# Three modulation blocks of the first mixer on VectorE, a fourth in the second mixer

## The chip, the cores and the metric

One NeuronCore of a Trainium2 chip runs the whole program, in one launch. The metric is the time of one execution in microseconds of device time, from the median of the runs. The engines are called TensorE (PE in the profile, PEld its weight loads), VectorE (DVE), ScalarE (ACT), GpSimd (POOL) and SyncE (SP, which here only issues transfers). Each takes its own instructions in the order of the program; they wait for one another through semaphores.

## The reference

A block of two layers over 512 latent tokens and 256 context tokens of 1024 channels, in float32. The first layer mixes the tokens by a bidirectional gated delta rule, the second by a short gated convolution; behind each stands a mixture of 32 experts. Ahead of every part the tokens are normalised and modulated: shift, scale and gate come from one matrix-vector product a layer, the "modulation", with a matrix of 1024 x 6144.

```python
def ada_params(cond, w, b):
    m = jax.nn.silu(cond) @ w + b
    return jnp.split(m[..., None, :], N_MOD, axis=-1)

def reference(x, c, ctx, c_ctx, ada_w, ada_b, ...):
    for i in range(DEPTH):
        sh_m, sc_m, gt_m, sh_f, sc_f, gt_f = ada_params(c, ada_w[i], ada_b[i])
        ...
        h = modulate(x, norm_mix[i], sh_m, sc_m)
        if kind == 0:
            y, yc = deltanet_mixer(h, hc, w_in_a[j], conv_a[j], ...)
        else:
            y = shortconv_mixer(h, w_in_b[j], conv_b[j], w_out_b[j], rows)
        x = x + gt_m * y
        hf = modulate(x, norm_ffn[i], sh_f, sc_f).reshape(b * s, d)
        x = x + gt_f * hier_moe(hf, router_g[i], router_e[i], w1[i], w3[i], w2[i]).reshape(b, s, d)
    return rmsnorm(x, final_norm)
```

The six vectors of a layer are three blocks of 2048 columns: block 0 is shift and scale of the mixer, block 1 the mixer's gate and the experts' shift, block 2 the experts' scale and gate. Block (l, b) is block b of layer l. Block (0, 0) is needed first and for both token kinds; it is not touched here. The other five are needed later: (0, 1) and (0, 2) at the end of the first mixer and in the first experts, (1, 0) at the entry of the second mixer, (1, 1) and (1, 2) at its end and in the last experts.

## The kernel before

The program is one long sequence: start-up (to about 60 us), phase A of the first mixer (projections of 32 "jobs" of 128 columns each, to about 400 us), its recurrence and output projection (to about 590 us), the first experts (to about 1090 us), the second mixer (about 1136 to 1360 us) and the last experts.

All weights come in units of 2 MB through rings of slots. `plan` writes the order of the units by hand, and `issue` starts a load on SP's queue as soon as the slot's last unit counts as used up; a load therefore waits on the engine that used the slot.

A job of phase A takes four columns' worth of a unit, splits 128 columns of the weights into a high and a low part (`split`: ScalarE writes `whi`, L637; GpSimd subtracts for `wlo`, L639), multiplies them in three passes with the tokens (`mm3`, L654, into the banks `pj` and `pc`), convolves the result along the tokens on VectorE and ScalarE (`job_conv`, L768 to L770) and, for k and v, turns it (`job_post`, L803, with sums of squares on ScalarE, L808). Between the matmuls of a job `work` puts in pieces of the "side work" of the delta rule: the matrices L (`lmat`, L897 to L908), the inverses of their diagonal blocks (`lanes`, on VectorE and GpSimd in turn: L931 and L932 step by step, then L948 and L949), and the whole inverses (`tmat`). There are three sets of lanes, one for each pair of token tiles. `norms` (L818) stands ahead of the first L.

In phase A the modulation of four blocks, (0, 1), (0, 2), (1, 0) and (1, 1), is done on TensorE (`ada_block`, L253): a unit is 256 rows of the matrix by 2048 columns, 8 matmuls with the condition as the stationary operand, which the profile shows as 16 records. `ada_at` gives the number of units at each job: 16 units over jobs 4 to 18, up to two at a job. A block's bias and its conversion to columns and rows follow (L260, `ada_tail`).

In the second mixer the fifth block, (1, 2), is done otherwise (`ada_unit`, L295 and L297, and `ada_sum`, L306): VectorE multiplies each part of 128 rows by its 128 conditions, one to a partition, and adds the products up; then a matmul with ones sums over the partitions. Its four units are taken at jobs 3 to 6.

The program is written in this order, but a scheduler with its own model of time may move instructions of one engine past each other; the order that results is shown below, at the places that matter.

Of the kernel before, what the change touches and what calls it, by code (L numbers as in the profile page):

```python
# [9 lines left out]
F32 = mybir.dt.float32  # L10
# [23 lines left out]
class Net:  # L34
# [10 lines left out]
    # ------------------------------------------------------------ constants  # L45
# [36 lines left out]
    def vectors(self, cp, pp):  # L82
        """Per-channel vectors, one channel per partition."""
# [29 lines left out]
        self.adab = self.ca.tile([128, 512], F32, name="adab")  # L113
        nc.vector.memset(self.adab, 0.0)
        self.grow = self.dr.tile([4, 2048], F32, name="grow")

    # ------------------------------------------------------------ ring of weights
    def plan(self):
        """All weights, in the order of their use, through rings of 2 MB units."""
        adas = [(0, 1), (0, 2), (1, 0), (1, 1), (1, 2)]  # L120
        adas, self.later = adas[:4], adas[4:]
        order = [("w_in_a", 4128, 2, 0)] + [("ada0", j) for j in range(4)]
        self.units = (2, 3, 0, 1, 4, 5, 6, 7)
        self.ada_at = [0] * 4 + [2, 2, 1, 0, 2, 1, 1, 1, 2, 1, 0, 0, 2, 1] + [0] * 14
        parts = [("ada",) + b + (j,) for b in adas for j in range(4)]
        order.append(("w_in_a", 4128, 3, 0))
        for i in range(4, 32):
            for _ in range(self.ada_at[i]):
                order.append(parts.pop(0))
            if i % 4 == 3 and i < 31:  # L130
                order.append(("w_in_a", 4128, self.units[i // 4 + 1], 0))
# [51 lines left out]
    def load_unit(self, pool, o, eng):  # L183
# [18 lines left out]
        if o[0] == "ada":  # L202
            _, l, b, j = o
            t = t.rearrange("p (k n) -> p k n", k=2)
            src = dap(I["ada_w"], l * D * 6 * D + j * 256 * 6 * D + b * 2048, [[6 * D, 128], [128 * 6 * D, 2], [1, 2048]])
# [6 lines left out]
        elif o[0] in ("w1", "w3") or o[0] == "w2" and o[2] < 30:  # L212
            # both experts of a pair, half of the parts k
# [17 lines left out]
    def free(self, i):  # L231
        """Unit i is used up, though some before it are not."""
# [3 lines left out]
    def next_unit(self, hold=0):  # L236
        """The next unit; all before it but the last `hold` are used up."""
# [1634 lines left out]
```

## Time and profile before

| | us |
|---|---|
| median of 3 runs | 1902.57 |
| lowest and highest run | 1897.57, 1904.13 |
| span of the profiled execution, from its first to its last instruction | 1893.7 |
| TensorE busy in it | 1716.9 (91%) |
| VectorE busy | 813.8 (43%) |
| ScalarE busy | 482.8 (25%) |
| GpSimd busy | 457.2 (24%) |

The span is the profiled execution's own time; what a run has besides (8.9 us from the span to the median of the runs) lies outside the first and last instruction. An engine's busy share is a mean over stages with different limits: with 91% TensorE is full in most of the mixers and mostly busy in the experts, where its matmuls keep pace with the transfers. The mean granted clock of TensorE is 0.961 of full speed.

### The profile page before, as it was taken

To read this page: it belongs to the slowest core of one execution; us is meant where nothing else is said; L and a number is where in the kernel's file an instruction comes from. 1 tells how busy PE (TensorE), PEld (TensorE's weight loads), DVE (VectorE), ACT (ScalarE), POOL (GpSimd) and SP (SyncE) were. 2 spreads that over 40 slices of the span, in tenths; PEclk is the share of its full clock that TensorE was granted. 3 is DMA by queue.
4 is the path that set the end of the run, shared out by engine and by line. 5 is a ranking of instruction groups with operands and counts; after the bars stand their busy time and mean duration, and the time that the engine had idled before them with its cause. 6 is when DMAs were issued, how large, how long until landed. Compare 5 with 4: busy or idle time off the path is not lost. (4 is left out here: it accounts for less than half of the span.)

```text
span 1893.7 us, 26630 instructions
## 1 busy us (share of the span) xinstructions
PE 1716.9 (91%) x10245; PEld 985.8 (52%) x10246; DVE 813.8 (43%) x1590; ACT 482.8 (25%) x886; POOL 457.2 (24%) x356
## 2 busy tenths in 40 slices
PE   5999978987987899998999988999799999999897
PEld 4766666776866443433343336688634344434332
DVE  5434877846764232322233237633513233323233
ACT  4465354423223111101011114223211111111012
POOL 1114464725310211211121103343112112111110
PEclk9999999998997899999999999999899999999999
DMA  9479975679928699999999963714689989999993
GB/s 330 187 239 337 314 215 141 169 174 269 247 80 319 273 419 420 420 420 420 420 419 392 388 238 110 276 40 178 235 344 420 420 331 410 419 420 420 420 418 133
DMA packets 178611, 579.67 MB, mean 306 GB/s; under 512 B 53409, under 2 KB 78162, under 8 KB 126210
## 3 DMA queue, kind: packets, MB, share of 16 engines
q1 hardware_dynamic: 157762, 437.81, 62.9%
q0 software_dynamic: 20672, 139.47, 18.1%
q8 instruction: 115, 1.88, 0.4%
q14 instruction: 62, 0.51, 0.1%
HBM read 550.86 MB, written 26.38 MB: 305 GB/s over the span
## 5 line engine op out<-in xcount | busy, mean ns | idle before, releaser
L1436 PE MATMUL pj<-w,hg 128*64 128x512 f32 x2048 | 485.8, 610 | 21.0 <-DMA w<-in_w 14.8
L1503 DVE TENSOR_TENSOR xs<-pj,xs 128x512 f32<-128x512 f32 x264 | 170.5, 687 | 361.2 <-PE pj L1502 357.4
L1436 PEld LDWEIGHTS pj<-w,hg 128*64 128x64 f32 x2048 | 153.7, 139 | 292.4 <-issue 246.0
L1464 PE MATMUL pj<-w,gT 128*64 128x512 f32 x960 | 212.6, 594 | 3.1 <-issue 1.6
L639 POOL TENSOR_TENSOR wlo<-w,whi 128x1024 fp32r<-128x1024 f32 x43 | 106.8, 2487 | 230.3 <-ACT whi L637 228.8
L1476 POOL TENSOR_TENSOR ylo<-g,yhi 128x512 fp32r<-128x512 f32 x56 | 70.8, 1264 | 298.1 <-ACT yhi L1475 298.1
L1464 PEld LDWEIGHTS pj<-w,gT 128*64 128x64 f32 x960 | 77.6, 137 | 117.1 <-issue 108.8
L1413 POOL DMA_INDIRECT hg<-hscr,gix x32 | 32.8, 1025 | 421.6 <-PEq L1576 330.6
L1471 DVE SCALAR_TENSOR_TENSOR g<-pj,wsl,gate 128x512 f32<-128x512 f32 x64 | 48.1, 751 | 182.7 <-PE pj L1464 111.1
L1501 PE MATMUL pj<-yhi,sel 128*128 128x512 f32 x264 | 118.1, 447 | 4.9 <-PEq L1576 4.2
L1453 ACT ACTIVATE gT<-tr 128x512 f32<-128x512 f32 x32 | 19.1, 597 | 400.9 <-PE tr L1451 400.9
L1501 PEld LDWEIGHTS pj<-yhi,sel 128*128 128x128 f32 x264 | 49.6, 188 | 122.2 <-issue 103.3
L1502 PE MATMUL pj<-ylo,sel 128*128 128x512 f32 x264 | 105.2, 398 | 3.1 <-POOL ylo L1476 3.1
L654 PE MATMUL pj<-w,whi 128*128 128x512 f32 x336 | 105.3, 393 | 0.6 <-ACT whi L637 0.6
L654 PE MATMUL pj<-hhi,wlo 128*128 128x512 f32 x224 | 93.3, 416 | 8.8 <-POOL wlo L639 7.1
L654 PE MATMUL pj<-hhi,whi 128*128 128x512 f32 x224 | 93.2, 416 | 8.0 <-DVE cv L770 5.8
L1475 ACT ACTIVATE yhi<-g 128x512 fp32r<-128x512 f32 x62 | 39.1, 630 | 223.0 <-DVE g L1471 223.0
L654 PE MATMUL pj<-hlo,whi 128*128 128x512 f32 x224 | 91.1, 407 | 0.0
L654 PEld LDWEIGHTS pj<-w,whi 128*128 128x128 f32 x336 | 63.8, 190 | 15.1 <-ACT whi L637 1.0
L637 ACT ACTIVATE whi<-w 128x1024 fp32r<-128x1024 f32 x53 | 55.3, 1052 | 55.1 <-PE pj L654 37.6
L654 PE MATMUL pj<-w,wlo 128*128 128x512 f32 x168 | 66.5, 396 | 0.0
L1426 ACT ACTIVATE hg<-tr,m 128x128 f32<-128x128 f32 x128 | 48.1, 456 | 57.4 <-PE tr L1422 57.4
(604 smaller groups left out, 2721.2 us busy)
## 6 DMA issues: line engine op xcount, KB each, us to landing
w<-in_w SPq DMA_DIRECT2D x130, 2048.0 KB
w<-in_w POOLq DMA_DIRECT2D x58, 2048.0 KB, 19.1
w<-in_ada_w SPq DMA_DIRECT2D x20, 2048.0 KB
w<-in_w_in_a SPq DMA_DIRECT2D x8, 2048.0 KB
w<-in_w_in_b SPq DMA_DIRECT2D x6, 2048.0 KB
w<-in_ada_w SPq DMA_DIRECT2D x8, 1024.0 KB
w<-in_w SPq DMA_DIRECT2D x8, 1024.0 KB
Y<-R SPq DMA_DIRECT2D x20, 256.0 KB
```

Of the source, the lines that this page charges most:

```text
L637: nc.scalar.activation(hi[:, :, :n], w, AF.Copy)
L639: (lo_eng or nc.gpsimd).tensor_tensor(lo[:, :, :n], w, hi[:, :, :n].bitcast(F32), op=OP.subtract)
L654: nc.tensor.matmul(out, n[j][0][:, k], n[j][1][:, k, a:b], start=(i == 0), stop=(i == 23))
L1426: nc.scalar.activation(hT[:, c], q, AF.Identity, bias=self.m8[:, l, 2, c:c + 1], scale=self.m8[:, l, 0, c:c + 1])
L1436: nc.tensor.matmul(ps[64 * x:64 * x + 64], hT[:, k, 64 * x:64 * x + 64], w[k // 4][:, x, k % 4], start=(k == 0), stop=(k == 7))
L1464: nc.tensor.matmul(py[n][64 * x:64 * x + 64], gT[:, k, 64 * x:64 * x + 64], w[h][:, x, k % 2, 512 * n:512 * n + 512], start=(k == 0), stop ...
L1471: nc.vector.scalar_tensor_tensor(y, py, wi, self.gate[:, 512 * n:512 * n + 512], op0=OP.mult, op1=OP.mult)
L1475: nc.scalar.activation(o[0][:, c], y, AF.Copy)
L1476: eng.tensor_tensor(o[1][:, c], y, o[0][:, c].bitcast(F32), op=OP.subtract)
L1501: nc.tensor.matmul(ps, s, yhi[:, c], start=True, stop=False)
L1502: nc.tensor.matmul(ps, s, ylo[:, c], start=False, stop=True)
L1503: nc.vector.tensor_tensor(self.xs[:, t, c], ps, self.xs[:, t, c], op=OP.add)
```

## The change

Blocks (0, 1), (0, 2) and (1, 0) are now summed on VectorE in phase A, in the manner of the second mixer's block: `ada_block` takes a unit of 512 rows by 1024 columns, multiplies its four parts of 128 rows into an accumulator `adacc` of 128x1024 (L254 the first, L256 the others), and after every second unit two matmuls with ones (`ada_ones`, L275) sum half of the block over the partitions. `ada_at` now has one piece at each of jobs 4 to 18, four units and the conversion of each block. Block (1, 1) joins (1, 2) in the second mixer, whose eight units are taken at jobs 3, 5, 7, 9, 10, 10, 15 and 17, and whose loads are interleaved with those of `w_in_b` in another order.

```diff
-        adas, self.later = adas[:4], adas[4:]
+        adas, self.later = adas[:3], adas[3:]
...
-        self.ada_at = [0] * 4 + [2, 2, 1, 0, 2, 1, 1, 1, 2, 1, 0, 0, 2, 1] + [0] * 14
-        parts = [("ada",) + b + (j,) for b in adas for j in range(4)]
+        self.ada_at = [0] * 4 + [1] * 15 + [0] * 13
+        parts = [x for b in adas for x in [("ada",) + b + (j,) for j in range(4)] + [None]]
...
-        for g in range(2):
-            order.extend(("w_in_b", 3072, u + g, 0) for u in (0, 2, 4))
-            if g == 0:
-                order.extend(("ada_w", 6144, 4 * b + u, l) for l, b in self.later for u in range(4))
+        later = [("ada_w", 6144, 4 * b + u, l) for l, b in self.later for u in range(4)]
+        order.extend(("w_in_b", 3072, u, 0) for u in (0, 2, 4))
+        order += later[:6]
+        order.extend(("w_in_b", 3072, u, 0) for u in (1, 3, 5))
+        order += later[6:]
...
+        self.place.update((o, "A") for o in later[4:])
...
-            t = t.rearrange("p (k n) -> p k n", k=2)
-            src = dap(I["ada_w"], l * D * 6 * D + j * 256 * 6 * D + b * 2048, [[6 * D, 128], [128 * 6 * D, 2], [1, 2048]])
+            t = t.rearrange("p (k n) -> p k n", k=4)
+            src = dap(I["ada_w"], l * D * 6 * D + j % 2 * 512 * 6 * D + b * 2048 + j // 2 * 1024, [[6 * D, 128], [128 * 6 * D, 4], [1, 1024]])
...
-    def ada_block(self, l, b, cp, sp, pp, tag):
+    def ada_block(self, l, b, cp, a):
         nc = self.nc
         ps = self.bank("ada")
         for j in range(4):
             w = self.next_unit()
-            for k in range(2):
-                for g in range(4):
-                    nc.tensor.matmul(ps[32 * g:32 * g + 32], self.sc[:, 2 * j + k, :], w[:, k, 512 * g:512 * g + 512],
-                                     start=(j == 0 and k == 0), stop=(j == 3 and k == 1), tile_position=(0, 32 * g))
+            for k in range(4):
+                f = self.sc1[:, 4 * (j % 2) + k:4 * (j % 2) + k + 1]
+                if j % 2 + k == 0:
+                    nc.vector.tensor_scalar(a, w[:, k], f, None, op0=OP.mult)
+                else:
+                    nc.vector.scalar_tensor_tensor(a, w[:, k], f, a, op0=OP.mult, op1=OP.add)
+            if j % 2:
+                self.ada_ones(ps, j - 1, a)
             if j < 3:
                 yield
...
+    def ada_ones(self, ps, g0, a):
+
+        for g in range(2):
+            self.nc.tensor.matmul(ps[32 * (g0 + g):32 * (g0 + g) + 32], self.ones[:, :32], a[:, 512 * g:512 * g + 512],
+                                  start=True, stop=True, tile_position=(0, 32 * (g0 + g)))
...
-                    if i0 <= i < i0 + 4 * len(self.later):
-                        j = i - i0
+                    for j in (j for j in range(8) if at[j] == i):
                         if j % 4 == 0:
                             acc = [wk.tile([128, 1024], F32, name="xn") for _ in range(2)]
-                        self.ada_unit(self.next_unit(3 + j), j, acc)
+                        self.ada_unit(self.next_unit(self.taken - t0), j, acc)
                         self.free(self.taken - 1)
-                        self.issue(self.taken - 4 - j)
+                        self.issue(t0)
```

How this moves instructions is seen at three places. Line numbers above about 330 are 14 larger in the changed program (L654 is L668, L769 and L770 are L783 and L784, L931 and L932 are L945 and L946, L949 is L963). A row ends in the shape that is written; x2 stands for two in a row.

On VectorE, just ahead of the second set of lanes (whose first step is the 128x2 row), before the change, where `cv` is a convolution and `TT` and `ltmp` belong to the first set:

```order
L949 TENSOR_REDUCE TT<-ltmp 128x4x8 x2
L769 SCALAR_TENSOR_TENSOR cv<-pc,V,cv 128x255
L770 SCALAR_TENSOR_TENSOR cv<-pc,V,cv 128x255
L769 SCALAR_TENSOR_TENSOR cv<-pj,V,cv 128x511
L1013 TENSOR_SCALAR Y<-Y 128x1024
L770 SCALAR_TENSOR_TENSOR cv<-pj,V,cv 128x511
```

and after it:

```order
L963 TENSOR_REDUCE TT<-ltmp 128x4x8
L784 SCALAR_TENSOR_TENSOR cv<-pc,V,cv 128x255
L783 SCALAR_TENSOR_TENSOR cv<-pj,V,cv 128x511
L256 SCALAR_TENSOR_TENSOR adacc<-w,V,adacc 128x1024
L784 SCALAR_TENSOR_TENSOR cv<-pj,V,cv 128x511
L963 TENSOR_REDUCE TT<-ltmp 128x4x8
L256 SCALAR_TENSOR_TENSOR adacc<-w,V,adacc 128x1024
L783 SCALAR_TENSOR_TENSOR cv<-pc,V,cv 128x255
L256 SCALAR_TENSOR_TENSOR adacc<-w,V,adacc 128x1024
L784 SCALAR_TENSOR_TENSOR cv<-pc,V,cv 128x255
L256 SCALAR_TENSOR_TENSOR adacc<-w,V,adacc 128x1024 x4
L945 TENSOR_TENSOR ltmp<-TT,Ll 128x2
```

The last unit of the third block stands among the last reductions of the first set and directly ahead of the second. Counted over the whole program's order, VectorE has 3 of L254 and 16 of L256 ahead of `norms`, 1 and 10 from there to the first set of lanes, 2 and 16 from there to the second, and none later in the first mixer; the other instructions between these landmarks are nearly the same in both programs (two convolutions more ahead of `norms`, two fewer behind it, one fewer ahead of the second set).

On TensorE, at the start of a job, before the change; `pj` is the bank of the projection's 512 latent tokens, `sc` the conditions (this is the last of the 16 units):

```order
L654 MATMUL pc<-hlo,whi 128x256
L796 MATMUL tr<-ident,cv 128x128
L253 MATMUL ada<-w,sc 32x512 x8
L654 MATMUL pj<-hhi,whi 128x512
L654 MATMUL pj<-hhi,wlo 128x512
```

and after it, the last pair of ones-matmuls, where the rows also show what an instruction waits for (a semaphore of the engine named, with 49 as a placeholder for the count):

```order
L668 MATMUL pc<-hlo,whi 128x256
L668 MATMUL pj<-hhi,whi 128x512 [waits Activation_49]
L275 MATMUL ada<-adacc,ones 32x512 [waits DVE_49]
L275 MATMUL ada<-adacc,ones 32x512
L668 MATMUL pj<-hhi,wlo 128x512 [waits Pool_49]
```

The eight matmuls that waited for no engine are replaced by two that wait for VectorE's sum; the projection's other matmuls are queued behind them.

On SP's queue, where the loads of phase A's weights stand between the side work's transfers (`Lscr` and `Ll` carry L to the lanes, `Y` the decays, `kscr` k), before:

```order
L810 DMA kscr<-tk 128x6x128 [waits Activation_49]
L228 DMA w<-in_ada_w 128x2x2048 [waits DMAHW1_49,PE_49]
L228 DMA w<-in_ada_w 128x2x2048 [waits DMAHW2_49,PE_49]
L810 DMA kscr<-tk 128x6x128 [waits DMAHW3_49,Activation_49]
L228 DMA w<-in_ada_w 128x2x2048 [waits DMAHW4_49,DMAHW1_49,PE_49]
```

and after:

```order
L228 DMA w<-in_w_in_a 128x8x512 [waits DMAHW0_49,DVE_49]
L922 DMA Lscr<-Y 128x1024 [waits DMAHW1_49,DVE_49]
L894 DMA Y<-R_89 64x1024 [waits DMAHW2_49,DMAHW1_49]
L894 DMA Y<-R_89 64x1024 [waits DMAHW3_49]
L228 DMA w<-in_ada_w 128x4x1024 [waits DMAHW4_49,DVE_49]
L922 DMA Lscr<-Y 128x1024 [waits DMAHW5_49,DVE_49]
L933 DMA Ll<-Lscr 16x32x32 [waits DMAHW6_49,PE_49]
```

Loads that waited for TensorE to be done with a slot now mostly wait for VectorE, that of the next `w_in_a` unit among them, and transfers of the side work stand behind them in the queue.

## Rows read from the trace of the kernel before

**Rows 1.** The page: the span, and the rate of transfers in 40 equal slices.

```profile
span 1893.7 us, 26630 instructions
GB/s 330 187 239 337 314 215 141 169 174 269 247 80 319 273 419 420 420 420 420 420 419 392 388 238 110 276 40 178 235 344 420 420 331 410 419 420 420 420 418 133
```

**Rows 2.** VectorE at `norms`, first and second lanes (start us, us).

```profile
167.51 0.45 DVE L818 RECIPROCAL rk<-rt 128x48 f32<-128x48 f32 x1 [4.97 <-ACT rt L817]
...
199.96 0.20 DVE L931 TENSOR_TENSOR ltmp<-TT,Ll 128x2 f32<-128x2 f32 x1 [0.79 <-DMA adab<-in_ada_b]
...
273.05 0.16 DVE L931 TENSOR_TENSOR ltmp<-TT,Ll 128x2 f32<-128x2 f32 x1 [2.71 <-DMA Tt<-lscr]
```

**Rows 3.** Stretches: PE, PEld, DVE, ACT, POOL busy, PEclk, DMA share, GB/s.

```profile
75.00:167.50 92.50, 88.26 (x575) 58.50 (x576) 39.59 (x72) 64.58 (x175) 21.40 (x13) 0.96 0.72 254
167.50:200.00 32.50, 32.50 (x291) 21.53 (x290) 21.96 (x59) 11.82 (x13) 13.55 (x9) 1.00 1.07 333
200.00:256.00 56.00, 45.30 (x287) 31.77 (x287) 52.38 (x78) 18.59 (x22) 30.67 (x20) 0.94 0.82 291
256.00:273.00 17.00, 15.71 (x108) 14.23 (x107) 5.92 (x9) 13.38 (x18) 13.13 (x9) 1.00 0.78 174
273.00:335.00 62.00, 53.09 (x593) 44.44 (x592) 46.53 (x75) 32.66 (x50) 32.89 (x21) 0.96 0.63 160
600.00:1090.00 490.00, 450.38 (x1983) 190.63 (x1984) 151.13 (x307) 63.18 (x128) 79.88 (x81) 0.96 0.97 400
```

**Rows 4.** Stretches of L253 alone: PE, PEld busy (records), PEclk, DMA, GB/s.

```profile
60.00:167.50 107.50, 20.78 (x144) 4.82 (x144) 0.97 0.66 234
167.50:200.00 32.50, 5.75 (x48) 1.33 (x48) 1.00 1.07 333
200.00:273.00 73.00, 7.86 (x64) 2.14 (x64) 0.95 0.81 264
```

**Rows 5.** Line L306, ones-matmuls: min/median/max ns; what TensorE waits for.

```profile
L306 PE MATMUL pj<-xn,ones x8: 592/606/617, 1192.6 to 1210.0; 128*32 128x512 f32 x8
...
  DVE xn L297: 6.4, 4
```

**Rows 6.** VectorE by form, 75 to 273 us: count, busy us, mean ns.

```profile
L769 DVE SCALAR_TENSOR_TENSOR cv<-pj,V,cv 128x511 f32<-128x511 f32 x18 | 13.4, 746 | 22.0 <-ACT cv L768 21.9
...
L769 DVE SCALAR_TENSOR_TENSOR cv<-pc,V,cv 128x255 f32<-128x255 f32 x9 | 4.3, 480 | 11.5 <-ACT cv L768 11.5
```

**Rows 7.** Lines L297 and L900: duration ns min/median/max.

```profile
L297 DVE SCALAR_TENSOR_TENSOR xn<-w,V,xn x28: 739/746/2880, 1170.8 to 1206.7; 128x512 f32<-128x512 f32 x28
...
L900 DVE TENSOR_SCALAR Y<-Y x6: 679/684/2755, 141.9 to 248.2; 128x1024 f32<-128x1024 f32 x6
```

**Rows 8.** The timeline: GpSimd and VectorE at 141 us (start us, us).

```profile
141.44 2.65 POOL L639 TENSOR_TENSOR wlo<-w,whi 128x1024 fp32r<-128x1024 f32 x1 [5.89 <-ACT whi L637]
...
141.88 2.75 DVE L900 TENSOR_SCALAR Y<-Y 128x1024 f32<-128x1024 f32 x1
```

**Rows 9.** Stretches of the second mixer, columns as in rows 3.

```profile
1168.00:1210.00 42.00, 38.75 (x164) 29.27 (x163) 38.43 (x42) 10.20 (x13) 15.94 (x8) 1.00 0.44 156
1210.00:1240.00 30.00, 30.00 (x139) 23.93 (x138) 10.01 (x15) 6.48 (x8) 11.29 (x5) 0.94 0.80 281
1240.00:1270.00 30.00, 30.00 (x134) 24.86 (x133) 7.86 (x9) 9.43 (x12) 12.35 (x6) 1.00 0.00 1
```

**Rows 10.** VectorE by form, 1160 to 1215 us, columns as in rows 6.

```profile
L297 DVE SCALAR_TENSOR_TENSOR xn<-w,V,xn 128x512 f32<-128x512 f32 x28 | 26.2, 968 | 0.3
L295 DVE TENSOR_SCALAR xn<-w,V 128x512 f32<-128x512 f32 x4 | 4.6, 1168 | 2.0 <-DMA w<-in_ada_w 2.0
```

**Rows 11.** TensorE's timeline at 247 us: start us, us, [idle before, its end].

```profile
247.37 0.79 PE L654 MATMUL pj<-hhi,wlo 128*128 128x512 f32 x1 [7.11 <-POOL wlo L639]
...
251.59 0.40 PE L654 MATMUL pj<-hlo,whi 128*128 128x512 f32 x1
```

**Rows 12.** A stretch behind that wait, columns as in rows 3.

```profile
247.40:251.00 3.60, 3.60 (x9) 2.83 (x10) 3.60 (x8) 1.06 (x1) 1.08 (x1) 0.50 0.66 255
```

More of the change, by code (lines that the diff above doesn't have):

```diff
@@ L128, in plan @@
             for _ in range(self.ada_at[i]):
-                order.append(parts.pop(0))
+                order.extend(x for x in (parts.pop(0),) if x)
             if i % 4 == 3 and i < 31:
@@ L250, in ada_block, with ada_bias @@
             w = self.next_unit()
-            for k in range(2):
-                for g in range(4):
-                    nc.tensor.matmul(ps[32 * g:32 * g + 32], self.sc[:, 2 * j + k, :], w[:, k, 512 * g:512 * g + 512],
-                                     start=(j == 0 and k == 0), stop=(j == 3 and k == 1), tile_position=(0, 32 * g))
+            for k in range(4):
[6 more added lines that the diff above has]
+                self.ada_ones(ps, j - 1, a)
             if j < 3:
                 yield
-        for g in range(4):
-            nc.sync.dma_start(self.adab[32 * g:32 * g + 2], dap(self.I["ada_b"], l * 6 * D + b * 2048 + 512 * g, [[0, 2], [1, 512]]))
-        row = sp.tile([128, 512], F32, name="adarow")
-        nc.vector.tensor_tensor(row, ps, self.adab, op=OP.add)
-        yield
-        self.ada_tail(l, b, row, cp)
+        row, bias = a[:, :512], a[:, 512:]
+        self.ada_bias(l, b, bias)
+        yield
+        nc.vector.tensor_tensor(row, ps, bias, op=OP.add)
+        self.ada_tail(l, b, row, cp)
+        yield
+    def ada_bias(self, l, b, bias):
+        for g in range(4):
+            self.nc.sync.dma_start(bias[32 * g:32 * g + 32], dap(self.I["ada_b"], l * 6 * D + b * 2048 + 512 * g, [[0, 32], [1, 512]]))
+    def ada_ones(self, ps, g0, a):
+        for g in range(2):
+            self.nc.tensor.matmul(ps[32 * (g0 + g):32 * (g0 + g) + 32], self.ones[:, :32], a[:, 512 * g:512 * g + 512],
+                                  start=True, stop=True, tile_position=(0, 32 * (g0 + g)))
     def ada_tail(self, l, b, row, cp):
@@ L301, in ada_sum @@
         nc = self.nc
-        for g in range(4):
-            nc.sync.dma_start(bias[32 * g:32 * g + 32], dap(self.I["ada_b"], l * 6 * D + b * 2048 + 512 * g, [[0, 32], [1, 512]]))
+        self.ada_bias(l, b, bias)
         ps = self.bank("pj")
-        for g in range(4):
-            nc.tensor.matmul(ps[32 * g:32 * g + 32], self.ones[:, :32], acc[g // 2][:, 512 * (g % 2):512 * (g % 2) + 512],
-                             start=True, stop=True, tile_position=(0, 32 * g))
+        for g in range(2):
+            self.ada_ones(ps, 2 * g, acc[g])
         nc.vector.tensor_tensor(row, ps, bias, op=OP.add)
@@ L478, in phase_a @@
         self.dump("hlo", hlo.bitcast(F32))
+        acc = wk.tile([128, 1024], F32, name="adacc")
         def adas_gen():
             for b in self.adas:
-                yield from self.ada_block(*b, cp, wk, pp, "ada")
+                yield from self.ada_block(*b, cp, acc)
         adag = adas_gen()
@@ L1732, in load @@
                     if m == 0:
-                        us[x] = self.next_unit(x)
-                    return self.split(us[x][:, :, 128 * m:128 * m + 128], wk, 128)
+                        us[x] = self.taken, self.next_unit(self.taken - t0)
+                    r = self.split(us[x][1][:, :, 128 * m:128 * m + 128], wk, 128)
+                    if m == 3:
+                        self.free(us[x][0])
+                        self.issue(t0)
+                    return r
                 jobs = [(g, m, x) for g in range(2) for m in range(4) for x in range(3)]
-                us.update(enumerate(self.us))
+                t0 = self.taken - 3
+                us.update((x, (t0 + x, u)) for x, u in enumerate(self.us))
                 sp = load(3)
@@ L1757, in mixer1 @@
                 ps, old = [], (0, *self.acc)
-                i0 = 3
+                at = (3, 5, 7, 9, 10, 10, 15, 17)
                 for i, (g, m, x) in enumerate(jobs):
@@ L1782, in mixer1 @@
                             self.ada_sum(l, b, acc, row, bias, cp)
-                    if i == i0 + 4 * len(self.later):
+                    if i == at[-1] + 1:
                         self.columns(1)
```

3 lines of the change are left out of this document (1 added, 2 removed).

## The prediction

> **What bounds the kernel now.** I read the span and the transfer rate first [rows 1]: 1893.7 us, with the transfers at 419 to 420 GB/s in long stretches. Between 600 and 1090 us the transfer engines are busy 0.97 of the time; there [rows 3] the weights of the first experts set the pace, and whatever the first mixer loses or gains ahead of that is passed on whole. So the question is when each mixer ends.
>
> The stage that changes most is the projections of the first mixer, about 60 to 400 us. I cut it at the side work's landmarks on VectorE, because that engine's program has the same landmarks after the change: the reciprocal of `norms` (167.5 us), the first step of the first set of 16x16 inverses (200.0) and of the second (273.0) [rows 2]. The busy times between them [rows 3] show two different limits. Up to 200 us TensorE is the limit: 88.3 of 92.5 us, then 32.5 of 32.5, while VectorE has 39.6 and 22.0. From 200 to 256 VectorE is the limit with 52.4 of 56 us, and TensorE waits (45.3). From 256 to 273 VectorE has only 5.9 of 17: it waits for transfers between the sets. From 273 to 335 neither is full (53.1 and 46.5 of 62).
>
> **What goes from TensorE.** The four modulation blocks are 256 records of L253, 34.4 us in all: 144 of them (9 units of 16 records) up to 167.5 us with 20.8 us, 48 with 5.8 up to 200, 64 with 7.9 up to 273 [rows 4], so 2.15 us a unit. What comes back is six pairs of ones-matmuls. A pair is 4 records of about 0.606 us [rows 5]; if they ran one after the other 2.4 us, if as closely as L253's (34.4 / 256 = 0.134 each) 0.5 us. I take 1.2, a middle value, 7 us in all. Net for TensorE: 27 us off.
>
> **What comes to VectorE.** Three blocks of 4 units of 4 instructions: 48, of which 6 are a multiplication alone (L254) and 42 a multiply-add (L256), each of 128x1024. No such multiply-add is in the trace. At 128x512 with both operands in SBUF it takes 0.746 us (median, minimum 0.739); at 128x511 and 128x255 from PSUM 0.746 and 0.480 [rows 6, 7]. The slope is 0.266 / 256 = 1.04 ns an element, which gives 0.746 + 513 x 1.04 = 1.28 us. The multiplication is priced at L900's 0.68 [rows 7]. Sum: 42 x 1.28 + 6 x 0.68 = 57.8 us without collisions.
>
> Collisions: a GpSimd subtraction of 2.65 us began at 141.44; the VectorE multiplication L900, which takes 0.68, began at 141.88 and lasted 2.75, until the other was done [rows 8]. In the second mixer, with GpSimd busy 15.9 of 42 us [rows 9], the 28 multiply-adds took 0.968 on average [rows 10], 0.22 over the median of 0.746. With GpSimd's 43.8 of 73 us between 200 and 273 I take 0.22 as the lower end and twice that, 0.44, as the upper. The rows agree with the Trainium skill, "SBUF — State Buffer", section "Who interferes with whom", which has VectorE and GpSimd hold one shared port pair as an exclusive lock. By that lock an instruction that arrives in a busy 0.60 of the time would wait half of 2.65 us on average, 0.8 us, which would put this price at 13 us for 16 instructions instead of my 3.5 to 7.
>
> **The sum, stage by stage.** The order of VectorE's instructions in the changed program says how many of the new ones stand between the landmarks: 3 multiplications and 16 multiply-adds up to `norms`, 1 and 10 up to the first set, 2 and 16 up to the second, none behind it.
>
> - To 167.5 us: TensorE is spared 20.8 and gets two pairs, 2.4: 18.4 us at most. VectorE gets 16 x 1.28 + 3 x 0.68 = 22.5, and has 52.9 idle: hidden. But a convolution on VectorE may now stand behind 1.28 us instructions, and ScalarE is at 64.6 of 92.5 and would be at 64.6 of some 75. Ends -18 and -5; I take -12, the middle.
> - To 200: VectorE gets 10 x 1.28 + 0.68 = 13.5 against 10.5 us idle, so about 3 us must show, and 10 x 0.22 = 2 of collisions: +5. The chain here (masks on GpSimd, products, store, load of the diagonal blocks) is in series with these instructions. Ends 0, since TensorE is spared 5.8, and +10.
> - To 273: VectorE gets 16 x 1.28 + 2 x 0.68 = 21.8 and 3.5 to 7 of collisions, 27 in the middle. Idle are 3.6 and 11.1 us [rows 3], 14.7; the idle before the second set is a chain of transfers, and the last 8 new instructions are put in it. I let 10 us of it hide: +17. Ends: +11 (all idle filled) and +22.
> - Behind 273: VectorE's order has no new instruction, and TensorE, which by the order is about one projection behind its place before, has 8.9 us idle up to 335. I take 0, with 3 either way.
>
> So the first mixer ends -12 + 5 + 17 = 10 us later (ends -10 and +30).
>
> The new waits: TensorE takes its instructions in order, and the ones-matmuls stand among the projections, so every projection behind a pair waits for VectorE's sums. The last pair stands within a projection and waits for the last multiply-adds ahead of the second set; it is part of the +17. On SP's queue the load of the next `w_in_a` unit now waits for VectorE's release of a slot where it waited for TensorE's, and stores and loads of the side work stand behind it. Transfers are spared 8 MB here, so I charge no time for that, and up to 8 us (one projection) if the load comes late.
>
> **Second mixer.** Four more units: 28 + 4 instructions, 26.2 + 4.6 = 31 us by [rows 10]; VectorE has 10.0 of 30 and 7.9 of 30 busy after 1210, while TensorE is full [rows 9]. They are spread over jobs 3 to 17. The 8 MB are 20 us at 420 GB/s, and the transfers there rest (share 0.00 from 1240 to 1270): hidden. Eight more records of ones-matmuls cost TensorE 1.2 x 2 = 2.4 us in a full stretch; the block done before now waits less (6.4 us of TensorE's waits on VectorE were in it [rows 5]). I take +2, ends -4 and +8.
>
> Together +12: 1893.7 becomes 1905.7. The median of the runs, 1902.57, lies 8.9 us above the profiled span, and I let that stand: 1914.6, rounded to 1914.5.
>
> **Rivals.**
> 1. VectorE hides all of it: its idle up to 273 us is 52.9 + 10.5 + 14.7 = 78 us against 57.8 new ones. Then TensorE's 27 us count in full: 1902.6 - 27 = 1876, or with ScalarE in the way about 1885. For: TensorE is full up to 200. Against: two thirds of that idle lie before 167.5, where only 22.5 of the 57.8 are asked for, and from 200 to 256 it is VectorE that is waited for. 0.24.
> 2. The gain up to 167.5 (18 rather than 12) and the loss up to 273 (11 to 17) cancel: 1902. 0.16.
> 3. Coupling in the lanes. At 240 us TensorE waited 7.11 us for one subtraction on GpSimd [rows 11], because GpSimd, in order, stood in the inverses, which alternate with VectorE. Each multiply-add between those steps holds VectorE 1.28 us, so GpSimd, the split of the next weights and the projection with it; and after that wait the first matmul took 0.79 us and a like one at 251.6 0.40; the granted clock was 0.50 over the nine matmuls behind the wait [rows 12], the lower of its two levels (1.2 and 2.4 GHz). Two or three more waits of 7 us are +15 to +20 on top of mine: 1932. It decides once the waits on GpSimd in 200 to 335 exceed TensorE's idle there, 20.9 us. 0.14.
> 4. Two SBUF operands cost double: the 1024 multiply-add then is 0.21 + 2 x 1.07 = 2.35 us, 42 x 1.07 = 45 more, of which 27 fall behind 167.5: 1942. The Trainium skill, "Vector Engine (DVE) Microarchitecture Reference", section "Points that are easy to get wrong", says that a scalar_tensor_tensor with two non-bf16 SBUF sources halves its throughput. The 0.746 us from SBUF beside 0.746 from PSUM speaks against it: 0.02.
>
> **How the numbers follow.** My case holds 0.44, and 1908 to 1926 for itself. Less than 0.3% (5.7 us) can't be told from no change here. Faster is rival 1: 0.24. Same is rival 2: 0.16. Slower is mine and rivals 3 and 4: 0.60. The range leaves out a tenth on either side: down into rival 1, 1886, and up past rival 3, 1936.
>
> **What would show it.** Right: `norms` at about 155 us, the first set at 193, the second at 283, VectorE over nine tenths busy between the last two. L256 at a median of 1.28 with a tail of over 2 us. TensorE's longest waits on VectorE at the ones-matmuls and on GpSimd's `wlo`. Wrong: the second set at or before 273; or a second mixer that is longer by over 8 us; or a stage behind the second set that gives back what was lost.

## The result, and the profile after

The changed kernel takes 1950.82 us (median of 4 runs, 1949.36 to 1952.77) beside 1900.07 of the kernel before in the same runs: ratio 1.0282, 95% interval 1.0257 to 1.0307. I had forecast slower, but by 12 us and with 1936 as the upper end; it is 51.

The page of the changed kernel, beside the table of before:

```profile
span 1951.0 us, 26270 instructions
PE 1716.6 (88%) x10021; PEld 995.5 (51%) x10022; DVE 900.5 (46%) x1669; ACT 482.8 (25%) x886; POOL 475.8 (24%) x356
```

TensorE lost 34.4 us of L253 [rows 4] and is busy for as long as before (1716.9); its mean granted clock fell from 0.961 to 0.938. VectorE has 87 us more.

The landmarks on VectorE's timeline (start us, us), to hold against [rows 2]; the second step is the first of the first set of lanes, the third that of the second set:

```profile
169.69 0.45 DVE L832 RECIPROCAL rk<-rt 128x48 f32<-128x48 f32 x1 [0.48 <-ACT rt L831]
...
205.66 0.15 DVE L945 TENSOR_TENSOR ltmp<-TT,Ll 128x2 f32<-128x2 f32 x1
...
303.76 0.16 DVE L945 TENSOR_TENSOR ltmp<-TT,Ll 128x2 f32<-128x2 f32 x1 [10.01 <-DMA T<-lscr]
```

So `norms` is 2.2 us later, the first set of lanes 5.7, the second 30.7. Between the two sets lies the moment at which the first set is done and SP stores it, before (first line) and after:

```profile
256.06 0.35 SPq L952 DMA_DIRECT2D lscr<-TT  x1
```

```profile
282.43 0.34 SPq L966 DMA_DIRECT2D lscr<-TT  x1
```

The first set took 76.8 us up to its store where it took 56.1, and from there to the second set 21.3 us passed where it was 17.0. The stretches between (columns as in [rows 3]):

```profile
75.00:169.70 94.70, 82.44 (x522) 61.72 (x522) 60.41 (x94) 66.25 (x178) 21.52 (x13) 0.94 0.55 183
169.70:205.70 36.00, 21.71 (x174) 15.62 (x175) 33.87 (x62) 8.95 (x9) 16.48 (x8) 0.74 0.73 214
205.70:293.80 88.10, 60.23 (x307) 47.32 (x305) 83.68 (x106) 35.52 (x41) 58.20 (x31) 0.79 0.65 221
293.80:303.80 10.00, 6.67 (x29) 4.51 (x29) 0.04 (x1) 0.00 (x0) 2.29 (x2) 1.00 0.73 125
303.80:360.80 57.00, 47.10 (x504) 40.13 (x505) 40.22 (x75) 26.74 (x44) 27.90 (x17) 0.82 0.66 168
```

The third number is VectorE (after PE and PEld): 33.9 of 36 and 83.7 of 88.1 us are full, then 10 us with nothing, then again as before. TensorE has 21.7 of 36 where it had 32.5 of 32.5. Its longest waits in 75 to 400 us (us in all, times, longest) are on VectorE's convolutions (L784), on GpSimd's squares of a convolution's result (L793) and on VectorE's products for L (L917):

```profile
PE pj L668 <- DVE cv L784: 23.7, 4, 9.1
PE pc L804 <- POOL cv L793: 14.1, 3, 7.0
PE pp L911 <- DVE Gm L917: 7.7, 2, 5.2
```

The ones-matmuls, which I had named as the new wait, waited 1.4 us in all for the sums.

The new multiply-adds cost what was priced, and a little for collisions; the six multiplications (L254) took nearly twice the 0.68 us that I had put (groups by form, count | busy us, mean ns):

```profile
L256 DVE SCALAR_TENSOR_TENSOR adacc<-w,V,adacc 128x1024 f32<-128x1024 f32 x42 | 61.2, 1457 | 0.4
L254 DVE TENSOR_SCALAR adacc<-w,V 128x1024 f32<-128x1024 f32 x6 | 7.9, 1309 | 8.7 <-PE tr L638 8.2 <-PE ada L275 0.5
```

Three more marks from the traces: the last projection of the first mixer ends at 434.3 us in place of 399.9; the first experts begin at 670.0 in place of 628.0; the second mixer's products take 133.0 in place of 125.0. So 42 us arise in the first mixer, 8 in the second. The two spans differ by 57.3, the medians by 51: the profiled execution of before was among its fastest. The rest, 6.7 us, lies behind the second mixer's products, where the change adds nothing (592.7 us before, 599.4 after; 591.9 to 600.0 in the other kernels with the whole modulation).

One sentence of the text ahead of the prediction is wrong: that 8.9 us lie outside the first and last instruction. The profiled execution after took 1952.77 us with a span of 1951.0, so 1.8 us lie outside; the rest of the 8.9 was the difference between runs.

### The profile page after: what moved, and what is told of

The parts are those of the page before. It is cut to its first block, busy times and chain, and to the rows that moved or that the text cites. A ratio compares the mean times of both kernels' runs of the same rounds, so it can differ in the third digit from the quotient of the medians.

```text
span 1951.0 us, 26270 instructions
## 1 busy us (share of the span) xinstructions
PE 1716.6 (88%) x10021; PEld 995.5 (51%) x10022; DVE 900.5 (46%) x1669; ACT 482.8 (25%) x886; POOL 475.8 (24%) x356
## 5 line engine op out<-in xcount | busy, mean ns | idle before, releaser
L1450 PE MATMUL pj<-w,hg 128*64 128x512 f32 x2048 | 484.3, 608 | 27.0 <-DMA w<-in_w 21.3
L1467 ACT ACTIVATE gT<-tr 128x512 f32<-128x512 f32 x32 | 19.1, 597 | 407.4 <-PE tr L1465 407.4
L668 PE MATMUL pj<-hhi,whi 128*128 128x512 f32 x224 | 95.6, 427 | 25.8 <-DVE cv L784 23.7
L668 PE MATMUL pj<-w,whi 128*128 128x512 f32 x336 | 106.1, 396 | 0.0
L668 PE MATMUL pj<-hhi,wlo 128*128 128x512 f32 x224 | 93.1, 416 | 0.0
L668 PE MATMUL pj<-hlo,whi 128*128 128x512 f32 x224 | 91.9, 410 | 0.0
L668 PEld LDWEIGHTS pj<-w,whi 128*128 128x128 f32 x336 | 64.2, 191 | 13.5
L668 PE MATMUL pj<-w,wlo 128*128 128x512 f32 x168 | 67.0, 399 | 0.8 <-POOL wlo L653 0.8
L668 PEld LDWEIGHTS pj<-hhi,whi 128*128 128x128 f32 x224 | 44.9, 201 | 39.3 <-issue 26.3
```

Source lines behind the costliest of these rows:

```text
L668: nc.tensor.matmul(out, n[j][0][:, k], n[j][1][:, k, a:b], start=(i == 0), stop=(i == 23))
L1450: nc.tensor.matmul(ps[64 * x:64 * x + 64], hT[:, k, 64 * x:64 * x + 64], w[k // 4][:, x, k % 4], start=(k == 0), stop=(k == 7))
```

## Experiments

In the table "job 12" is the start of its matmuls, "second lanes" the first step of the second set, "last job" the end of the last projection, "experts" the first matmul of the first experts, "second mixer" the length of its products; all are us in the one profiled execution of each kernel (that of before is about 5 us shorter than the median of its runs; by the stretch behind the second mixer, which is among the shortest, little of that lies in these marks). "The recurrence ended" is the end of its last product with the state, 522.4 before and 564.0 in the changed kernel. A ratio to the kernel before with its interval stands where the whole time can be compared. In the other five the modulation is not the reference's, the tokens are routed differently, and only the marks up to "experts" are read.

| kernel | job 12 | second lanes | last job | experts | second mixer | ratio |
|---|---|---|---|---|---|---|
| before | 181.2 | 273.0 | 399.9 | 628.0 | 125.0 | 1 |
| changed | 180.7 | 303.8 | 434.3 | 670.0 | 133.0 | 1.0282 (1.0257 to 1.0307) |
| narrow | 177.8 | 288.3 | 392.8 | 633.4 | | |
| half | 180.7 | 303.4 | 423.3 | 658.1 | | |
| noload | 165.7 | 313.3 | 429.0 | 660.8 | | |
| psum | 180.7 | 300.5 | 429.5 | 665.7 | | |
| nothing | 164.6 | 275.6 | 369.3 | 619.8 | | |
| movefour | 180.8 | 280.7 | 407.0 | 639.1 | 133.1 | 1.0096 (1.0068 to 1.0125) |
| tensor3 | 183.4 | 271.1 | 401.9 | 640.5 | 135.0 | 1.0130 (1.0095 to 1.0166) |
| spread | 186.1 | 289.1 | 397.3 | 637.4 | 125.1 | 1.0046 (1.0030 to 1.0062) |
| one | 179.0 | 289.2 | 407.7 | 643.2 | 125.1 | 1.0111 (1.0090 to 1.0132) |
| early | 218.0 | 311.3 | 432.1 | 665.8 | 135.1 | 1.0253 (1.0212 to 1.0293) |
| earlype | 218.2 | 302.0 | 444.6 | 678.0 | 125.1 | 1.0269 (1.0228 to 1.0310) |
| tail | 181.0 | 303.9 | 434.1 | 668.9 | 133.0 | 1.0270 (1.0223 to 1.0317) |
| bias | 180.4 | 302.5 | 431.8 | 665.3 | 132.3 | 1.0268 (1.0224 to 1.0313) |

**narrow: VectorE's work cut to 32 columns.** The multiplication of L254 is cut likewise, and the rest of the accumulator is set to zero at the start.

```diff
-                    nc.vector.scalar_tensor_tensor(a, w[:, k], f, a, op0=OP.mult, op1=OP.add)
+                    nc.vector.scalar_tensor_tensor(a[:, :32], w[:, k, :32], f, a[:, :32], op0=OP.mult, op1=OP.add)
```

> The 48 VectorE multiplications of the first mixer are cut to 32 of 1024 columns (the rest of the sums is left out); loads, slots, ones-matmuls and waits stay, and the second mixer is that of the changed kernel. Theory 'occupancy' (VectorE's 61 + 7 us of new instructions, in order ahead of the convolutions and of the side work, cost the 42 us of the first mixer): the first mixer comes back to before or 5 to 20 us under it, since TensorE is spared 27; the whole takes about 1895 to 1915, of which 10 to 14 are the second mixer and the last experts. Theory 'loads' (the next w_in_a unit waits in its slot and on SP's queue for VectorE's place in its order, not for the work): the first mixer stays at least 20 us longer than before, the whole at 1925 or more, and w_in_a's load for job 12 is still issued after 170 us.

The recurrence ended at 528.4 (before 522.4, changed 564.0): 35.6 of 41.6 us came back. The load for job 12 was issued at 166.4. Occupancy holds for most; but the mixer is 6 us longer than before, where I had expected it at before or 5 to 20 us under it, with TensorE spared 25 us. At the second lanes 15.5 of 30.7 us came back.

**half: 512 of 1024 columns.** The same edit with 512.

> The 48 multiplications of the first mixer take 512 of 1024 columns (half of the sums is left out). With 32 columns its recurrence ended 6.0 us behind before, with 1024 41.6. If the cost is the time that they hold VectorE (0.75 of 1.28 us, so half of it gone), the recurrence ends 20 to 28 us behind. If the first few microseconds were hidden and the rest not, or the other way (a threshold), under 14 or over 34.

The recurrence ended at 551.2, 28.8 behind: a little over the range for "half of it gone". But half the columns are not half the time here, since the multiply-adds met GpSimd more often. The groups of narrow, then of half:

```profile
L256 DVE SCALAR_TENSOR_TENSOR adacc<-w,V,adacc 128x32 f32<-128x32 f32 x42 | 17.2, 410 | 0.6
L254 DVE TENSOR_SCALAR adacc<-w,V 128x32 f32<-128x32 f32 x6 | 1.9, 310 | 4.8 <-PE tr L285 4.2 <-DMA grow<-adacc 0.5
```

```profile
L256 DVE SCALAR_TENSOR_TENSOR adacc<-w,V,adacc 128x512 f32<-128x512 f32 x42 | 46.4, 1105 | 2.0 <-DMA w<-in_ada_w 1.6
L254 DVE TENSOR_SCALAR adacc<-w,V 128x512 f32<-128x512 f32 x6 | 4.0, 664 | 0.8 <-PE ada L275 0.8
```

So VectorE is held for 19.1, 50.4 and 69.1 us, and the recurrence ends 6.0, 28.8 and 41.6 us behind: 0.73 us for each us in the first step and 0.68 in the second, much the same, with no sign of a threshold. Followed back to no time at all, this line gives 8 us ahead of before. That is one trace each, and half's second lanes are as late as the changed kernel's (303.4): there VectorE waited 13 us for a bias, just ahead of them.

**noload: the same instructions on a tile that is there already.** `h` is the tile of the tokens' high part, in the shape of a unit.

```diff
-                order.extend(x for x in (parts.pop(0),) if x)
+                parts.pop(0)
...
-            w = self.next_unit()
+            w = h
```

> The 12 units of the first mixer's modulation are not loaded (24 MB left out); the same 48 VectorE instructions of 128x1024 read another tile in SBUF instead, so their sums are not the modulation's. Slots are then free for w_in_a early. Theory 'occupancy': it stays near the changed kernel, 1935 to 1950, with TensorE still waiting 20 us and more for VectorE's convolutions between 200 and 330. Theory 'loads': 1900 to 1915, the first mixer near its old length.

Occupancy again: experts at 660.8, 9 us ahead of the changed kernel and 33 behind before, though with 73.3 us on VectorE (of the expected waits, TensorE had 14 us on convolutions and 11 on the sums between 200 and 330). But it shows what the loads do. Here the load for jobs 12 to 15 is issued at 122.2 and job 12 starts in time, with the modulation's transposes (L286 here) still among its matmuls:

```profile
122.16 0.38 SPq L228 DMA_DIRECT2D w<-in_w_in_a  x1
```

```profile
165.36 0.60 PE L286 MATMUL tr<-ident,adacc 128*128 128x128 f32 x4
165.71 0.49 PE L669 MATMUL pj<-hhi,whi 128*128 128x512 f32 x1
```

In the changed kernel job 12 starts 15 us later. Four engines' timelines there (start us, us) give the chain, a multiply-add, the load that waited for it, the split that waited for the load, the matmul:

```profile
170.12 1.27 DVE L256 SCALAR_TENSOR_TENSOR adacc<-w,V,adacc 128x1024 f32<-128x1024 f32 x1
...
171.42 0.37 SPq L228 DMA_DIRECT2D w<-in_w_in_a  x1
...
179.56 2.00 ACT L651 ACTIVATE whi<-w 128x1024 fp32r<-128x1024 f32 x2 [7.96 <-DMA w<-in_w_in_a]
...
180.66 0.80 PE L668 MATMUL pj<-hhi,whi 128*128 128x512 f32 x1
```

The multiply-add at 170.12 ended at 171.39 and freed the slot; in VectorE's order it stood behind `norms`, which waited for ScalarE. Job 11 had started at 158.0, 15.8 us ahead of before (173.8): nearly all that job 11 had gained was lost in this wait.

**psum: no collisions.**

```diff
-                    nc.vector.scalar_tensor_tensor(a, w[:, k], f, a, op0=OP.mult, op1=OP.add)
+                    nc.vector.scalar_tensor_tensor(a2, w[:, k].rearrange("p (c n) -> p c n", c=2), f, z, op0=OP.mult, op1=OP.add)
```

Here `z` is the zeroed bank, spread over both halves.

> The multiply-adds take their second operand from a zeroed PSUM bank instead of the accumulator in SBUF (the sum over parts is left out), so they have one SBUF input; their length and places stay. Theory 'collisions' (waiting out GpSimd, and GpSimd waiting for them, made the cost): no multiply-add of over 1.35 us, GpSimd's subtractions near 2.40 again, and 15 to 30 us back, 1920 to 1935. Theory 'occupancy': the L256 group falls from 61 to 54 us, and the whole by 3 to 8 us, 1943 to 1948.

The group fell to 53.5 us, each at 1.27:

```profile
L258 DVE SCALAR_TENSOR_TENSOR adacc<-w,V,ada 128x1024 f32<-128x1024 f32 x42 | 53.5, 1273 | 0.6 <-DMA w<-in_ada_w 0.3
```

The experts began 4.3 us earlier than in the changed kernel. Collisions are 4 us of 42 as these kernels stand; that they were the main cost has fallen. The 4 is a net figure: the first set was stored 12.3 us earlier (270.1), but 30.4 us passed from there to the second set in place of 21.3, with three loads of `w_in_a` in SP's queue between them; such loads come up again under spread.

**nothing: neither loads nor products.**

```diff
-            w = self.next_unit()
-            for k in range(4):
-                f = self.sc1[:, 4 * (j % 2) + k:4 * (j % 2) + k + 1]
...
+        nc.gpsimd.memset(acc, 0.0)
```

> Neither the loads nor the products of the three blocks are there in the first mixer (both left out); ones-matmuls, biases and conversions stay. What taking the blocks off TensorE is worth when nothing takes their place. Theory 'TensorE bounds the first mixer': its recurrence ends 25 us or more ahead of before (at or under 498 us in the trace). Theory 'the lanes bound it from 200 us on, whatever TensorE gains ahead': job 12 starts at about 165 us in place of 181, but the second set of lanes is less than 8 us earlier than 273 and the recurrence ends between 510 and 525. Only the first mixer is read, since the experts' routing changes with the modulation.

This settles the ceiling for these places. Projections end 30.6 us earlier, but the recurrence at 513.8, 8.6 earlier, where the line of narrow, half and the changed kernel leads too; the second set of lanes starts at 275.6, no earlier than before, and `norms` at 169.9, as late as with the work. Even at no cost at all the blocks' absence is worth 8 us here: what TensorE gains ahead of the lanes is not passed on by them.

**movefour, tensor3 and spread: the move and the places, without VectorE.** In movefour only the fourth block moves (12 units on TensorE at before's places); tensor3 has the units one to a job from job 4 besides, at jobs 4 to 15, which is near the changed kernel's places but without its gaps at jobs 8 and 13; spread is the kernel before with its 16 units one to a job. The edit of spread:

```diff
-        self.ada_at = [0] * 4 + [2, 2, 1, 0, 2, 1, 1, 1, 2, 1, 0, 0, 2, 1] + [0] * 14
+        self.ada_at = [0] * 4 + [1] * 16 + [0] * 12
```

> Only the fourth block moves to the second mixer, as in the change; the other three stay on TensorE in the first mixer as before (12 units at jobs 4 to 12). The second mixer and the last experts should be 10 to 14 us longer, as in the changed kernel, if the move itself is their cause. The first mixer is spared 4 units, 8.6 us of TensorE: if TensorE's work bounds it there, -5 to -9, the whole 1903 to 1910; if the lanes on VectorE bound it, 0 to -3, the whole 1908 to 1915.

> The changed kernel's places (12 units one to a job from job 4, the fourth block in the second mixer), with the three blocks' sums on TensorE in place of VectorE. Against the changed kernel it has 25.8 us of TensorE for 68 us of VectorE. Theory 'VectorE's time': the recurrence ends within 12 us of before (522), as in the run that moved only the fourth block (533), and 30 us ahead of the changed kernel. Theory 'the place of the loads': 545 us or later.

> The kernel before with one thing changed: its 16 units of the first mixer stand one to a job at jobs 4 to 19 (all on TensorE, all work done). Theory 'VectorE's time': the pattern costs nothing, the recurrence ends within 4 us of 522, the whole 1894 to 1904. Theory 'the place of the loads' (units one to a job put the next w_in_a behind a slot that comes free late, whoever frees it): w_in_a for job 12 is issued later than 164 us, job 12 starts 8 us or more late, and the recurrence ends 10 to 25 us behind.

Movefour is at 1916.28 (before 1897.32): 8.1 us in the second mixer (10 to 14 expected with the last experts, which added none), but 11 in the first, where I had expected a gain; its recurrence ended at 533.2. Tensor3 is at 1919.94 (before 1898.42) with the recurrence at 537.1, 14.7 behind: not within 12, not at 545, so both theories have a part. Its second lanes are not late; what it loses comes in the recurrence, which took 135.2 us behind the last job in place of 122.5, and why stays open. Spread costs 9 us with nothing changed but the places (recurrence at 531.9, 9.5 behind; its load for job 12 was issued at 162.2, no later than before, yet job 12 started 4.9 us later and the second lanes 16.1).

The 16.1 us have a cause in the trace. The first set was done 1.2 us later than before, but two loads of `w_in_a` of 2 MB each stood in SP's queue ahead of the loads for the second set, and SP waited 7.4 us for them (the last line: us in all, times, longest):

```profile
257.27 0.34 SPq L952 DMA_DIRECT2D lscr<-TT  x1
...
263.15 1.01 SPq L228 DMA_DIRECT2D w<-in_w_in_a  x2
...
279.96 0.81 SPq L972 DMA_DIRECT2D Tt<-lscr  x2
```

```profile
SPq L972 <- DMA w<-in_w_in_a: 7.4, 1, 7.4
```

From the store of the first set to the second set 31.9 us passed in place of 17.0. All fifteen traces fall in with this: 13.6 to 17.0 us with no load of `w_in_a` issued in between (before, narrow, noload, nothing, tensor3, early, earlype), 20.5 to 25.3 with one (changed, half, movefour, tail, bias), 29.8 to 31.9 with two (spread, one) or three (psum).

Tensor3 to the changed kernel is VectorE in place of TensorE, with places that differ a little: 29.5 us at the experts, 31 in the medians.

The two stretches of the projections behind `norms` show the exchange (columns as in [rows 3]), tensor3 first, then the changed kernel:

```profile
167.70:402.00 234.30, 211.13 (x1928) 162.77 (x1927) 172.04 (x296) 101.48 (x144) 126.69 (x79) 0.92 0.68 193
```

```profile
169.70:434.00 264.30, 205.04 (x1825) 160.49 (x1825) 205.38 (x322) 101.62 (x141) 141.84 (x77) 0.85 0.66 191
```

VectorE's 33.3 us more are 30 us more of length. TensorE is spared work and still has 205 busy, at a granted clock of 0.85 in place of 0.92.

**one, early and earlype: other places for VectorE's blocks.** One puts a single block on VectorE at jobs 4 to 7; early puts all 12 units at jobs 4 to 11, none in the lanes; earlype does that and keeps the fourth block in the first mixer. The edit of early:

```diff
-        self.ada_at = [0] * 4 + [1] * 15 + [0] * 13
+        self.ada_at = [0] * 4 + [2, 2, 2, 2, 2, 2, 2, 1] + [0] * 20
```

> Only block (0, 1) goes to VectorE (16 instructions, at jobs 4 to 7, ahead of norms), the other three stay on TensorE and the second mixer is that of before. TensorE is spared 8.6 less 2.4 us. With nothing in the blocks' place the recurrence ended 8.6 us earlier at most; for a fourth of that, with VectorE half idle in that stage: -3 to +3 us, the whole 1893 to 1903. If VectorE's work costs wherever it stands: +10 or more.

> The same work as the changed kernel, but the 12 units of the first mixer stand two to a job at jobs 4 to 11 instead of one to a job at 4 to 18, so that VectorE has no multiply-add between the first and the second set of lanes, and w_in_a for job 12 has its load free of VectorE's later work. Theory 'occupancy in the lanes': the second set starts at about 275 to 285 in place of 304, the first mixer is 20 to 30 us shorter than in the changed kernel, the whole 1920 to 1930. If the cost is the sum of VectorE's work wherever it stands, the first set of lanes starts later by what the second gains, and the whole stays within 8 us of 1951.

> Three blocks on VectorE at jobs 4 to 11 as in the run before, the fourth stays in the first mixer on TensorE (at jobs 11 to 15) and the second mixer is that of before. Theory 'occupancy in the lanes' with 8 us for the second mixer's move: 8 us less than the run before plus 2 to 8 for TensorE's four units, 1908 to 1922. Rival, the fourth block's loads collide with the side work's: over 1925.

All three missed what I had thought likelier: one took 1918.67, early 1948.42 and earlype 1952.20. In early the ring decides: with seven modulation units (in the changed kernel four) ahead of it, the `w_in_a` unit of jobs 8 to 11 gets its slot at 151.1 (changed 104.4), and job 8 starts at 160.7 in place of 134.7.

```profile
151.10 0.37 SPq L228 DMA_DIRECT2D w<-in_w_in_a  x1
```

From the second lanes on it has lost 38 us of 273, as the changed kernel 31. It took the instructions out of the lanes and put a 26 us wait ahead of them, so its whole time doesn't say what the lanes alone cost; earlype has the same wait. The stretch from the first set to the second does say something: with no new instruction in it, it takes 76.7 us in early and 67.8 in earlype, beside 73.1 before and 98.1 in the changed kernel. One lost 15 us at the experts (before 1898.48). Its second set is 16.2 us late with no new instruction between the sets: 9.7 us of that it had at the first set, the first set itself was 6.3 us shorter than before, and the transfers to the second took 12.8 us more, with two loads of `w_in_a` among them. So what VectorE's 20.6 us cost there can't be told apart from the places.

**tail and bias: the second mixer.** On the changed kernel's timeline VectorE's first multiplication of the fifth unit waits for its load, the sum of the first block (L320) stands behind it, and TensorE's transposes wait for the sum:

```profile
1268.03 2.07 DVE L309 TENSOR_SCALAR xn<-w,V 128x512 f32<-128x512 f32 x1 [8.09 <-DMA w<-in_ada_w]
...
1270.80 0.68 DVE L320 TENSOR_TENSOR u<-pj,y 128x512 f32<-128x512 f32 x1
...
1271.53 1.12 PE L285 MATMUL tr<-ident,u 128*128 128x128 f32 x4 [5.05 <-DVE u L320]
```

Tail writes the conversion one job later; bias loads the bias early, so that the sum's place is ahead of the fifth unit. The edit of bias, in part:

```diff
+                        if j % 4 == 1:
+                            bias = wk.tile([128, 512], F32, name="adb", bufs=1)
+                            self.ada_bias(*self.later[j // 4], bias)
```

> The changed kernel, with the conversion of a block in the second mixer (transposes on TensorE that waited 5.05 us for VectorE's sum) put one job later. If that wait is what the move costs there, the second mixer's products are 4 to 5 us shorter (129 us in place of 133) and the whole 1945 to 1948; if it is the added ones-matmuls and the clock, no change, 1949 to 1953.

> The changed kernel, with the bias of a block of the second mixer loaded into a tile of its own two units earlier, by which VectorE's sum of the block (L319) stands ahead of the next unit's first multiplication (L309), which waited 8.09 us for its load. Theory 'behind a late load': TensorE's wait of 5.05 us at the transposes goes, the second mixer's products take about 128 us in place of 133. Theory 'the added work alone': the wait only changes its name and 133 stays.

Tail changed nothing: the scheduler put the transposes where they had been, and the wait of 5.1 is still there. Bias took that wait away (job 12 of this mixer starts 8 us earlier, counted from the first product), and the products still take 132.3; TensorE now waits for the split of the next `w_in_b`:

```profile
PE pj L667 <- ACT whi L650: 5.3, 1, 5.3
PE pj L667 <- POOL wlo L652: 2.5, 2, 1.6
```

The wait changed its name, but what is behind it is not "the added work alone" either: TensorE had 4.2 us of ones-matmuls here, half of it new. That the loads are late in this stage is seen; that fewer of them would give the 8 us back is shown only by the kernels that keep the fourth block in the first mixer (125.1).

## Why the prediction was wrong, step by step

What failed is the overlap. Of some 65 us of new work on VectorE, collisions included, the prediction let 22 show (the +5 and the +17) and hid the rest in VectorE's idle time, and it counted 12 us of TensorE's relief as a gain. The runs show about 0.7 us of delay for each us that VectorE is held (narrow, half, changed), which is some 50 for its 69.1, and a gain of 8 to 9 for the relief (nothing): 41.6 at the end of the recurrence. The steps one by one, measured at the landmarks, are +2.2, +3.5, +25.0 and +11.3, 42.0 in all, for -12, +5, +17 and 0:

- *Durations*: right but for L254. L256 has a median of 1.276 (forecast 1.28), a pair of ones-matmuls 1.22 (7.33 us for six, forecast 1.2), collisions on L256 8 us in all (psum: 61.2 to 53.5). L254 took 1.309 on average (forecast 0.68), 3.8 us more for the six. The exclusion of rival 4 was right too: the 2.35 us that the rule of the Trainium skill, "Vector Engine (DVE) Microarchitecture Reference", section "Points that are easy to get wrong", would give is not what the trace shows.
- *"To 167.5: -12"*: failed as a step of its own, measured +2.2. The step held that what TensorE is spared brings `norms` forward. My own excerpt of the order said that two more convolutions stand ahead of `norms`; I left their two projections unpriced. VectorE's new work is not in it: without any, in nothing, `norms` is at 169.9. The 15.8 us gained at job 11 went into the wait for job 12's weights. Of that wait I had named the cause (the load behind VectorE's release of a slot) and priced it "no time, up to 8 us"; it was 15 (noload).
- *"To 200: +5"*: measured +3.5, but with two projections fewer in the stretch and job 12 late, so the step was right by luck: with the multiplications cut to 32 columns (narrow) the stretch is longer still, 37.7 us for 36.0.
- *"To 273: +17"*: mis-sized, measured +25.0. The idle time did hide about what I had let it: six of the 18 new instructions (9.7 us) ran behind the first set's last step, and VectorE still idled 10.01 us after them, waiting for transfers. But the other 12 (18.2 us) stand ahead of that step, and the first set took 20.7 us longer; so the chain of transfers that follows it began that much later as a whole. The chain itself took 4.3 us more, with a load of `w_in_a` in SP's queue that did not stand there before; that term was not in the sum.
- *"Behind 273: 0"*: failed, measured +11.3 up to the experts (42.0 less 30.7). TensorE was one projection behind by the order, and the 8.9 us of idle did not take it up: the last job ended 34.4 late where the third set of lanes was stored 26.7 late (406.9 for 380.3), and the recurrence behind it went from 122.5 to 129.7 us.
- *Second mixer, +2*: mis-sized, measured +8.0, the end of its range. The transfers that "rest" there did not help: VectorE waited 8.09 us for the load of the fifth unit. Which term gives the 8 us is not shown; bias moved the wait and left the length.
- *Places in the ring*: not in the sum at all. With the sums on TensorE, the places and the move cost 12.5 us at the experts (tensor3), 9.4 by other places alone in the kernel before (spread). Spread's second set waits behind two loads of `w_in_a`; the changed kernel's exact places were not tried with TensorE alone.

By tensor3, then, of the 51 us about 31 are VectorE in place of TensorE and 20 to 22 the move and the places, some 8 of them in the second mixer; by narrow 35.6 of the first mixer's 41.6 go when VectorE is held for 19.1 us in place of 69.1. Rival 1 has fallen (nothing, at no cost at all, gains 8), and with it rival 2, which needed that gain; of rival 3 the coupling was right, through VectorE's convolutions and the load rather than through GpSimd's `wlo`, whose waits are not among the longest. None of the kernels tried is faster than before.

## What to carry to other kernels

Idle time hides work only if the work stands inside it. Where an engine waits for a chain of transfers that begins when it has finished something, work behind that moment is hidden, and work ahead of it moves the whole chain. Before pricing what an engine is spared, ask what the next limit gives for it at best (here 8.6 us of 34), by a run that leaves the work out. And where weights come through a ring of few slots, whoever frees a slot is on the path of the next load, with everything that stands ahead of it in its order; and a large load that comes into the same queue ahead of small urgent transfers holds them up.

## What the runs showed of the hardware

- In the long stretches in which TensorE waited most, its granted clock was lower. It is a mean over its two levels (1.2 and 2.4 GHz): 0.74 in 169.7 to 205.7, where TensorE was idle for 14 of 36 us, and 0.79 in the next 88, where it was idle for 28; before it was 1.00 without idle time and 0.94 with 11 of 56 us [rows 3]. It is not so in every stretch: the 10 us from 293.8 had 1.00 with 6.7 busy. With 34.4 us removed and 9.4 of ones-matmuls added, its busy time in the whole program is the same, 1716.6 beside 1716.9.
- With one SBUF operand none of this kernel's 42 multiply-adds shows the tail that they had with two: 1.273 us on average and 1.282 at most, beside 1.457 and 3.316. The Trainium skill, "SBUF — State Buffer", section "Who interferes with whom", says that a VectorE instruction with two SBUF inputs contends with a GpSimd instruction that reads SBUF, and one with at most one such input does not; this trace agrees.
- Loads of 2 MB in a queue hold up the transfers behind them: SP waited 7.4 us for two of them in spread, and the step from the first to the second set of lanes took 13.6 to 17.0 us with none in between, 20.5 to 25.3 with one and 29.8 to 31.9 with two or three.
